# Second head pair's two weight sums: an accumulating DMA into a second load of one operand in place of VectorE additions

## The chip, the cores and the metric

The kernel runs on one core of one Trainium2 chip. A core has a matrix engine (TensorE, PE in the profile), three engines for element-wise work (VectorE or DVE, ScalarE or ACT, GpSimd or POOL), an engine that only issues transfers (SyncE or SP), and 16 DMA engines that move data between device memory and the core's on-chip memory. The metric is device time in microseconds (us) of one execution. It was measured in three runs of the kernel before: 846.02 us in the middle, 844.99 at the lowest, 846.65 at the highest.

## The reference

Two encoder layers over 512 tokens of 1024 channels, in float32. Both are: RMS norm, one wide input projection, an attention mixer, a gate, an output projection, and the residual added. Layer A, where the change stands, has dilated sliding-window attention with three dilation groups, merged by their softmax denominators:

```python
def mixer_a(hn, w_in, w_out, q_gain, k_gain, t5_bias):
    proj = hn @ w_in
    qkv = proj[..., :n_qkv].reshape(b, s, N_DIL_GROUPS, 3, N_HEADS, HEAD_DIM)
    gate = proj[..., n_qkv:]
    for g, (window, dilation) in enumerate(DILATED_PAIRS):
        q = rms_norm(qkv[:, :, g, 0], q_gain[g])
        k = rms_norm(qkv[:, :, g, 1], k_gain[g])
        v = qkv[:, :, g, 2]
        o, lse = dilated_group_attention(q, k, v, t5_bias[...], dilation, reach)
        ...
    alpha = jax.nn.softmax(jnp.stack(lses), axis=0)
    y = jnp.sum(alpha[..., None] * jnp.stack(outs), axis=0)
    y = y.reshape(b, s, BRANCH_WIDTH) * jax.nn.silu(gate)
    return y @ w_out
```

Inside `dilated_group_attention` the logits are `q k^T * scale + bias`, where the bias is a table over relative positions. Layer B does the same kind of work with a two-dimensional neighbourhood; it is not touched.

## The kernel before

**Weights.** The kernel's 16 heads are worked in eight pairs; `hc` counts them from 0. All projection weights lie in one packed array `in_w`. They come into on-chip tiles called `wraw`, 128 x 1024 float32 (512 KB), of which there are eight (`SLOTS`). Such a load is called a raw here. A raw is worked in two pieces of 512 columns, called jobs. For each job ACT casts the piece into a high part `wh`, then DVE or POOL subtracts it from the raw and makes the low part `wl`, and PE multiplies in three passes (`wh` by the high part of the activations, `wl` by the high part, `wh` by the low part). That is `splits()`, which runs a few jobs ahead of PE.

**The sums.** For the pairs 1 to 7 a part of the projection is done with products of sums, so that seven block products do the work of eight. Four weight blocks `b11`, `b21`, `b12`, `b22`, each of two raws (index 0 and 1), enter as they are and in these sums: `b11 += b12`, then `t2 = b11 + b22` (with `b11` already holding its sum), then `b12 += b22` and at last `t2 += b21`. The activations have sums of their own, `mixed`, with a high and a low part `mix_h` and `mix_l`. A sum with `+=` is a DMA that POOL issues with `accum_op=ALU.add` (`Plan.add`): it reads the operand from `in_w` and adds it into the `wraw` tile. The sum `t2 = b11 + b22` is a DVE addition of two tiles into a third (`Plan.sum`), 128 x 1024.

**The plan.** `Plan.mixed(hc)` writes down, for one pair, which raws are used at which job and at which job each sum is to be issued. `Plan.loads` then gives every raw that has an offset in `in_w` a job at which SP loads it: `lead` (12 jobs here) ahead of its first use, or later, when all eight slots are taken, at the job behind the last use of the raw whose slot comes free. Where a tile is to be written again, the loading DMA waits until the last reader of the slot has ended. The pair `hc == 1` is called `late` and has an order of its own (`b11`, gate, `b21`, `b11` again, `t2`, `b22`, `b12`, v, `t2` again).

**What sets the order.** PE's instructions stand in the order in which the program is written. The other engines are ordered by a scheduler at build time, except where the program holds an order. Each engine then works its list strictly from front to back: an instruction that waits holds up all behind it, and so does a DMA on the engine that issues it. SP issues the loads (`load`) and also the loads of the attention bias:

```python
def bias_a(hc):
    e0 = wk.tile([P, 2, 256], F32, tag="e0", name="e0", bufs=1)
    e12 = wk.tile([P, 4, 224], F32, tag="e12", name="e12", bufs=1)
    for hd in range(2):
        h = 2 * hc + hd
        syn.dma_start(e0[:, hd, :], ...)
        for g in range(2):
            syn.dma_start(e12[:, 2 * hd + g, :], ...)
```

These six transfers per pair (`e` in the profile, read from `l_d` in device memory) are stated in the order head 0, head 1. For the pair 0 they are needed when the attention's logits (`log`) are there: DVE adds the bias to the logits and keeps their extremes in `minima`, tile by tile, first for head 0 and then for head 1. After that come exponentials on ACT, transposes, and the values `vt`, which PE transposes (`tp`). All of pair 0's attention runs beside the projection of pair 1, whose weight sums are the ones that the change touches.

Two further small loads matter: `oh`, a one-hot table, with which PE makes the bias table (`pl`), and the stores `l_d` of that table, both on SP.

Of the kernel before, what the change touches and what calls it, by code (L numbers as in the profile page):

```python
# [46 lines left out]
def tile_hybrid_encoder(  # L47
# [49 lines left out]
    vec, act, pol, syn = (Ordered(e) for e in (nc.vector, nc.scalar, nc.gpsimd, nc.sync))  # L97
# [82 lines left out]
    class Plan:  # L180
# [28 lines left out]
        def add(self, at, dst, off):  # L209

            dst.used(at)
            src = lambda: w[:, off : off + dst.cols]
            self.sums.setdefault(at, []).append(
                lambda: pol.dma_start(dst.tile, src(), accum_op=ALU.add)
            )

        def mixed(self, hc):
            b, j = hc * A_HC, len(self.jobs)
            b11, b21, b12, b22 = ([self.raw(b + 2048 * n + 1024 * i) for i in range(2)] for n in range(4))
            gate = self.raw(b - A_HC + 1152 * KT)  # L220
            v = self.raw(b - A_HC + 1024 * KT)
            t2 = [self.raw(None) for _ in range(2)]
            late = hc == 1
            order = (b11, gate, b21, b11, t2, b22, b12, v, t2) if late else (b11, gate, b21, v, b11, t2, b22, b12, t2)
            for part in order:
                for raw in part if isinstance(part, list) else [part]:
                    self.use(raw, 128 if raw in (gate, v) else 512)
            for i in range(2):
                self.add(j + 3 + 2 * i, b11[i], b12[i].off)
                self.sum(j + (9 if late else 11) + 2 * i, t2[i], b11[i], b22[i], vec)  # L230
                self.add(j + 15 + 2 * i, b12[i], b22[i].off)
                self.add(j + (17 if late else 19) + 2 * i, t2[i], b21[i].off)

# [58 lines left out]
    def splits():  # L292
        casts, queue, due = [], [], plan.loads(lead)
        for at, (raw, c, step, n) in enumerate(plan.jobs):
            first = at - start_jobs
            pool[0] = [0, 1] if first < 16 else [1, 2] if at < mixed_jobs else [2, 5]
            for r in due.get(at, ()):
                load(r)
            for add in plan.sums.get(at, ()):
                add()  # L300
            casts.append((cast(raw.tile[:, c : c + step], step), n))
            if len(casts) > 1:
                done, m = casts.pop(0)
                queue.append((*rest(*done), m))
            if len(queue) > 4:
                yield queue.pop(0)
        done, m = casts.pop(0)
        queue.append((*rest(*done), m))
        yield from queue
# [94 lines left out]
    def squares(v, ss, i, ns, on_act=True):  # L404
        sq = wk.tile([P, 512], F32, tag="sq", name="sq")[:, : ns * 64]
        if on_act:
            act.activation(sq, v, AF.Square)
        else:
            pol.tensor_mul(sq, v, v)

        def add():
            vec.tensor_reduce(
                ss[:, i * ns : (i + 1) * ns], sq.rearrange("p (a b) -> p a b", b=64), axis=AX.X, op=ALU.add
            )

        later_on(800, add) if held[0] else add()
# [270 lines left out]
    def main_a(hc):  # L687
# [50 lines left out]
        for n, acc, first, put in ((0, c, True, put_v), (1, b, True, put_u), (3, c, False, put12), (2, b, False, put22)):  # L738
            yield "mix", n
            yield from product(acc, mixed(n), first, put, ("q", hc - 1) if n == 0 else None)  # L740
# [794 lines left out]
```

## Time and profile before

| what | value |
|---|---|
| median of the runs (lowest to highest) | 846.02 us (844.99 to 846.65) |
| the profiled execution's own time | 846.23 us |
| its span in the trace | 844.3 us |
| PE busy | 827.9 us, 98% |
| DVE, ACT, POOL busy | 632.8, 507.7, 292.0 us |
| granted TensorE clock | 1.00 |
| loads and other transfers on SP's queue (q1) | 108.39 MB, 41.8% of 16 engines' span |
| accumulating DMAs on POOL's queue (q0) | 42 of 512 KB, 22.02 MB, 15.2% |

Times in the rows are microseconds from the start of the span. A row of a timeline has start, duration, engine, line, operation, output and inputs with their shape and, in square brackets, how long the engine was idle before and on what it waited. Nearly every row has line 85, because a helper records each call there; the names of the tiles tell them apart, and numbers of buffers are left out. "SPq" and "POOLq" are the queues' issuing work, not the transfer itself. A row of windows gives a stretch, then its length, then busy time of PE, PEld (weight load), DVE, ACT and POOL, the clock, the share of the DMA engines and GB/s. A row of the DMA view has 40 equal slices with the busy share of the 16 engines in tenths, and under it the GB/s. A line of a queue has packets, MB and the share of 16 engines' time.

### The profile page before, as it was taken

What the parts mean: (1) busy time and instruction counts of PE and PEld (TensorE: products, weight loads), DVE (VectorE), ACT (ScalarE), POOL (GpSimd) and SP (SyncE); (2) the same over time, 40 slices, a digit from 0 to 9 for tenths busy, and PEclk for the clock granted to TensorE, in tenths of its full rate; (3) what the DMA queues carried; (4) which work ended last, traced back from release to release, by engine and by line L of the source; (5) the groups of instructions that cost most, each with busy time, mean ns of one, the idle gap of its engine ahead of it and who ended that gap; (6) DMA issues with size and microseconds to landing.
All of it is one profiled execution on the core that took longest, in us unless ns stands there. A gap on an engine that the chain in (4) does not pass through costs nothing.

```text
span 844.3 us, 18126 instructions
## 1 busy us (share of the span) xinstructions
PE 827.9 (98%) x6611; PEld 684.9 (81%) x6611; DVE 632.8 (75%) x1653; ACT 507.7 (60%) x1066; POOL 292.0 (35%) x259
## 2 busy tenths in 40 slices
PE   8999999999999999999999999999999999999998
PEld 6877878878877878878888887789998898889786
DVE  7899997897996886896796876466668767776742
ACT  7657766846846846747747738454546664666440
POOL 5042343543533533533533524213123222322201
PEclk9999999999999999999999999999999999999999
DMA  9426765676687776785676554473265456634212
GB/s 339 144 57 165 194 154 150 141 168 197 133 181 211 159 174 173 164 210 134 157 180 176 105 183 144 152 235 114 91 191 164 130 145 180 179 129 114 85 51 101
DMA packets 56169, 131.97 MB, mean 156 GB/s; under 512 B 7184, under 2 KB 24528, under 8 KB 55952
## 3 DMA queue, kind: packets, MB, share of 16 engines
q1 hardware_dynamic: 49456, 108.39, 41.8%
q0 software_dynamic: 6048, 22.02, 15.2%
q8 instruction: 52, 0.85, 0.4%
q10 hardware_dynamic: 576, 0.41, 0.2%
q14 instruction: 37, 0.30, 0.1%
HBM read 111.73 MB, written 11.72 MB: 146 GB/s over the span
## 4 chain that ended last, share of the span: by engine, by line
PE 76%; ACT 9%; DVE 8%; issue 3%; DMA 3%; POOL 1%; SPq 0%; DVEq 0%; ACTq 0%; POOLq 0%
PE acc L324 63%; PE log L324 5%; PE o L324 4%; ACT p L85 4%; PE tp L328 3%; DVE wl L85 2%; ACT wh L85 1%; DVE na L85 1%; DMA wraw<-in_w 1%; DVE rawq L85 1%; DMA yr<-y_d 1%; ACT rawk L85 1%; DVE gt L85 1%; DVE p L85 1%; DMA pt<-in_xt 1%
## 5 line engine op out<-in xcount | busy, mean ns | idle before, releaser
L85 POOL TENSOR_TENSOR wl<-wraw,wh 128x512 fp32r<-128x512 f32 (+1 forms) x153 | 198.2, 1296 | 434.5 <-PE acc L324 223.2
L85 ACT CAST wh<-wraw 128x512 fp32r<-128x512 f32 (+1 forms) x360 | 209.3, 593 | 194.1 <-PE acc L324 154.9
L85 DVE TENSOR_TENSOR wl<-wraw,wh 128x512 fp32r<-128x512 f32 (+1 forms) x207 | 158.3, 768 | 44.5 <-PE acc L324 33.4
L324 PE MATMUL acc<-wh,hn_h 128*128 128x384 f32 (+1 forms) x488 | 185.5, 380 | 2.9 <-DVE gt L85 1.7
L324 PE MATMUL acc<-wl,hn_h 128*128 128x384 f32 (+1 forms) x488 | 177.2, 363 | 3.1 <-DVE wl L85 3.1
L324 PE MATMUL acc<-wh,hn_l 128*128 128x384 f32 (+1 forms) x488 | 176.9, 362 | 0.0
L85 ACT ACTIVATE p<-p,mn 128x256 f32<-128x256 f32 (+2 forms) x248 | 137.6, 584 | 32.3 <-DVE mn L85 32.3
L324 PEld LDWEIGHTS acc<-wh,hn_h 128*128 128x128 f32 x488 | 91.7, 188 | 21.4 <-issue 7.0
L324 PEld LDWEIGHTS acc<-wl,hn_h 128*128 128x128 f32 x488 | 91.9, 188 | 12.1 <-DVE wl L85 4.9
L324 PEld LDWEIGHTS acc<-wh,hn_l 128*128 128x128 f32 x488 | 91.6, 188 | 9.5
L324 PE MATMUL acc<-wh,mix_h 128*128 128x512 f32 x224 | 89.2, 398 | 0.0
L324 PE MATMUL acc<-wl,mix_h 128*128 128x512 f32 x224 | 87.6, 391 | 0.0
L324 PE MATMUL acc<-wh,mix_l 128*128 128x512 f32 x224 | 87.4, 390 | 0.0
L324 PE MATMUL acc<-hn_h,wh 128*128 128x512 f32 x192 | 79.0, 412 | 0.3 <-ACT rawb L85 0.2
L324 PE MATMUL acc<-hn_h,wl 128*128 128x512 f32 x192 | 75.1, 391 | 0.0
L324 PE MATMUL acc<-hn_l,wh 128*128 128x512 f32 x192 | 75.0, 391 | 0.0
L85 DVE STREAM_TRANSPOSE pt<-p 128x512 f32<-128x512 f32 (+1 forms) x60 | 40.6, 687 | 23.7 <-ACT p L85 23.6
L85 DVE TENSOR_REDUCE ss<-sq 128x4 f32<-128x256 f32 (+1 forms) x96 | 46.1, 501 | 11.0 <-POOL sq L85 5.9
L324 PE MATMUL acc<-y_h,wh 128*128 128x512 f32 x128 | 51.9, 406 | 0.5 <-ACT gt L85 0.5
L324 PEld LDWEIGHTS acc<-wh,mix_h 128*128 128x128 f32 x224 | 42.1, 188 | 10.0 <-issue 1.6
L324 PE MATMUL acc<-y_h,wl 128*128 128x512 f32 x128 | 50.0, 391 | 0.0
L324 PE MATMUL acc<-y_l,wh 128*128 128x512 f32 x128 | 49.9, 390 | 0.0
(148 smaller groups left out, 1361.5 us busy)
## 6 DMA issues: line engine op xcount, KB each, us to landing
wraw<-in_w SPq DMA_DIRECT2D x95, 512.0 KB
wraw<-in_w POOLq DMA_DIRECT2D x42, 512.0 KB, 7.0
wraw<-in_w SPq DMA_DIRECT2D x38, 384.0 KB
pt<-pt SPq DMA_DIRECT2D x106, 64.0 KB
td<-tr SPq DMA_DIRECT2D x24, 224.0 KB
pt<-td SPq DMA_DIRECT2D x24, 224.0 KB
e<-l_d SPq DMA_DIRECT2D x32, 112.0 KB
e<-l_d SPq DMA_DIRECT2D x16, 128.0 KB
```

Of the source, the lines that this page charges most:

```text
L85: m = f(*args, **kw)
L324: nc.tensor.matmul(o, l, r, **kw)
L328: nc.tensor.transpose(o, i, ident)
```

## The change

For the pair 1 alone, `t2` is no longer an empty tile into which DVE writes the sum. It is given the offset of `b22`, so SP loads `b22` a second time, straight into `t2`'s tile. Then an accumulating DMA on POOL's queue adds `b11` (which holds `b11 + b12`) to it. The source of that DMA is a tile in on-chip memory, not `in_w`: `add` takes a raw instead of an offset for that. The other six pairs keep the DVE sum.

```diff
         def add(self, at, dst, off):
 
             dst.used(at)
-            src = lambda: w[:, off : off + dst.cols]
+            if isinstance(off, Raw):
+                off.used(at)
+                src = lambda: off.tile
+            else:
+                src = lambda: w[:, off : off + dst.cols]
             self.sums.setdefault(at, []).append(
                 lambda: pol.dma_start(dst.tile, src(), accum_op=ALU.add)
             )
...
-            t2 = [self.raw(None) for _ in range(2)]
             late = hc == 1
+            t2 = [self.raw(b22[i].off if late else None) for i in range(2)]
...
             for i in range(2):
                 self.add(j + 3 + 2 * i, b11[i], b12[i].off)
-                self.sum(j + (9 if late else 11) + 2 * i, t2[i], b11[i], b22[i], vec)
+                if late:
+                    self.add(j + 9 + 2 * i, t2[i], b11[i])
+                else:
+                    self.sum(j + 11 + 2 * i, t2[i], b11[i], b22[i], vec)
                 self.add(j + 15 + 2 * i, b12[i], b22[i].off)
                 self.add(j + (17 if late else 19) + 2 * i, t2[i], b21[i].off)
```

Since `b22` is no longer an operand of the sum at job `j + 9`, its first use is at its own jobs, from `j + 18`. The plan's loads shift with that. With `j = 16`, counted in jobs: before, `b22[0]` and `b22[1]` are loaded at 13 and 17, `b12[0]` and `b12[1]` at 25 and 27. After, `t2[0]` and `t2[1]` are loaded at 13 and 15, `b12[0]` and `b12[1]` at 19 and 23, and `b22[0]` and `b22[1]` at 25 and 27, of which the last takes the slot that `b21[1]` leaves after job 25.

On SP, in the stretch from the loads ahead of `oh` to the bias of pair 0 (`e`) and the loads behind it, the program before has:

```order
L85 DMA wraw<-in_w 128x1024 x5
L85 DMA oh<-in_onehot 32x896
L85 DMA wraw<-in_w 128x1024
L85 DMA l_d<-mk 16x384 x4
L85 DMA l_d<-mk 16x512
L85 DMA wraw<-in_w 128x1024 x2
L85 DMA e_730<-l_d 128x1x256
L85 DMA e_731<-l_d 128x1x224 x2
```

And the changed program, in the same stretch:

```order
L85 DMA wraw<-in_w 128x1024 x6
L85 DMA oh<-in_onehot 32x896
L85 DMA wraw<-in_w 128x1024
L85 DMA l_d<-mk 16x384 x4
L85 DMA l_d<-mk 16x512
L85 DMA wraw<-in_w 128x1024 x3
L85 DMA e_732<-l_d 128x1x256
L85 DMA e_733<-l_d 128x1x224 x2
```

One weight load more stands ahead of `oh`, and one more ahead of the six loads of `e`: behind `l_d` there are now `b12[1]`, `b22[0]` and `b22[1]`, where `b12[0]` and `b12[1]` were.

On POOL, around the issue of the accumulating DMAs of pair 1, the difference of the two programs is:

```order
 L85 TENSOR_TENSOR mix_l<-mixed,mix_h 128x1024
 L85 TENSOR_TENSOR hn_l<-pt,hn_h 128x512
-L85 DMA wraw<-in_w 128x1024 x2
+L85 DMA wraw<-in_w 128x1024
+L85 DMA wraw<-wraw 128x1024 x2
+L85 DMA wraw<-in_w 128x1024
 L85 TENSOR_TENSOR wl<-wraw,wh 128x512
 L85 DMA wraw<-in_w 128x1024 x2
```

The two new DMAs (`wraw<-wraw`) stand between `b11[1] += b12[1]` and `b12[0] += b22[0]`, which followed each other before; the three accumulations of `t2 += b21` and `b12[1] += b22[1]` still come behind the next `wl`.

On DVE, in the stretch of pair 1's `wl` pieces, two rows go, the two sums; around the first of them the difference is:

```order
 L85 SCALAR_TENSOR_TENSOR rs<-na,rs 128x16
 L85 TENSOR_TENSOR rawk<-rawk,rs 128x256
-L85 TENSOR_TENSOR wraw<-wraw 128x1024
 L85 TENSOR_TENSOR wl<-wraw,wh 128x512
 L85 TENSOR_TENSOR mixed<-mixed,pt 128x1024
```

The `wl` now follows directly on the key rows' scaling (`rawk`). The rest of DVE's list keeps its order, and so do the lists of ACT and PE.

## The prediction

> **What bounds the kernel now.** I read the page's busy table first, then TensorE's (PE's) waits around the change.
>
> ```profile
> PE 827.9 (98%) x6611; PEld 684.9 (81%) x6611; DVE 632.8 (75%) x1653; ACT 507.7 (60%) x1066; POOL 292.0 (35%) x259
> ...
> PE acc L324 <- DVE wl L85: 1.3, 1, 1.3
> PE tp L328 <- ACT vt L85: 0.7, 1, 0.7
> ```
>
> PE is busy for 827.9 of 844.3 us, so the time is PE's work plus its few waits. The last two rows are all its waits between 30 and 160 us, where the two sums stand: 1.3 us for a `wl` (the low part of a weight piece, made by VectorE, DVE), then 0.7 us at 112 us. The timelines of PE, DVE and ACT show the first:
>
> ```profile
> 73.59 0.50 PE L324 MATMUL acc<-wl,hn_h 128*128 128x512 f32 x1 [1.31 <-DVE wl L85]
> ...
> 67.64 1.22 DVE L85 TENSOR_TENSOR wraw<-wraw 128x1024 f32<-128x1024 f32 x1
> 68.77 0.69 DVE L85 TENSOR_TENSOR wl<-wraw,wh 128x512 fp32r<-128x512 f32 x1
> 69.37 1.22 DVE L85 TENSOR_TENSOR mixed<-mixed,pt 128x1024 f32<-128x1024 f32 x1
> 70.51 0.76 DVE L85 TENSOR_TENSOR rawk<-rawk,rs 128x256 f32<-128x256 f32 x2
> 71.71 1.23 DVE L85 TENSOR_TENSOR mix_l<-mixed,mix_h 128x1024 fp32r<-128x1024 f32 x1 [0.45 <-ACT mix_h L85]
> 72.85 0.68 DVE L85 TENSOR_TENSOR wl<-wraw,wh 128x512 fp32r<-128x512 f32 x1
> 73.79 1.22 DVE L85 TENSOR_TENSOR wraw<-wraw 128x1024 f32<-128x1024 f32 x1
> 84.81 0.69 DVE L85 TENSOR_TENSOR rawq<-acc,rawk 128x512 f32<-128x512 f32 x1 [1.44 <-PE acc L324]
> ...
> 70.63 1.05 ACT L85 CAST mix_h<-mixed 128x1024 fp32r<-128x1024 f32 x1 [5.15 <-DVE mixed L85]
> ```
>
> DVE works without a gap from the first sum (67.64) to the `wl` of 72.85 that PE waits for; the 0.45 us for `mix_h` hangs on DVE's own `mixed` (69.37), so it moves with the rest. The second sum (73.79) stands behind that `wl`, and DVE waits for PE at 84.81.
>
> **The change, part by part.**
>
> *The two DVE sums go.* The first pushes the `wl` of 72.85 by 68.77 − 67.64 = 1.13 us. Without it PE waits 1.31 − 1.13 = 0.18 us: a gain of 1.13 us, 1.31 at most. The second frees DVE in a stretch that ends in a wait for PE, so I cost it at nothing.
>
> *Two accumulating DMAs come* (`t2 += b11`), on POOL's queue.
>
> ```profile
> 62.62 1.78 POOL L85 DMA_DIRECT2D wraw<-in_w  x2
> 78.91 2.18 POOL L85 TENSOR_TENSOR wl<-wraw,wh 128x512 fp32r<-128x512 f32 x1 [14.52 <-ACT wh L85]
> 81.39 1.76 POOL L85 DMA_DIRECT2D wraw<-in_w  x2 [0.30 <-POOL wl L85]
> 84.75 0.87 POOL L85 DMA_DIRECT2D wraw<-in_w  x1 [0.30 <-POOL wl L85]
> ...
> 79.49 0.65 ACT L85 CAST wh<-wraw 128x512 fp32r<-128x512 f32 x1
> ...
> DMA to landing us min/median/max: 5.7/7.7/9.0
> ...
> q1 hardware_dynamic: 49456, 108.39, 41.8%
> q0 software_dynamic: 6048, 22.02, 15.2%
> ...
> wraw<-in_w POOLq DMA_DIRECT2D x42, 512.0 KB, 7.0
> ```
>
> The row of landing times is that of POOL's DMAs between 55 and 95 us. The new ones go between the two issues of 62.62. Issuing costs POOL 0.9 us each; the second must also wait for the sum in `b11[1]` to land, 62.62 + 5.7 to 7.7 = 68.3 to 70.3, and `b12[0] += b22[0]` is queued behind it. POOL then has nothing until 78.91 (14.52 us idle), which hides both. ACT's cast of the second `t2` is that of 79.49, 78.4 with the gain; issued at 69 to 70 and 7.7 to 9.0 us under way, the sum lands at 77 to 79, which is about in time.
>
> On the 16 DMA engines an accumulation costs 15.2% × 844.3 / 42 = 3.06 us. Its source is now SBUF instead of HBM, which no row shows: as low as a plain load, 41.8% × 844.3 us × 0.524 / 108.39 MB = 1.7 us, or as high as twice the row, 6.1 us. I take 3.06: the destination and the adding there are those of the row, only the source is another.
>
> *The second load of `b22` moves other loads.* `t2` now loads early, where `b22` did, and `b22` itself is first used at its own jobs, nine jobs later, so its loads go down SP's order.
>
> ```profile
> 29.79 0.42 SPq L85 DMA_DIRECT2D oh<-in_onehot  x1
> 38.49 0.33 SPq L85 DMA_DIRECT2D wraw<-in_w  x1
> 65.69 8.08 SPq L85 DMA_DIRECT2D e<-l_d  x6
> ...
> L85 SPq DMA_DIRECT2D wraw<-in_w x5: 328/328/351, 65.1 to 91.6; - x5
> ...
> 46.03 1.68 PE L324 MATMUL pl<-oh,t 32*16 32x384 f32 x6
> ```
>
> `oh` comes behind the load that waited until 38.49: issued at 38.8, it has 7.2 us until PE reads it at 46.03. That is hidden (plain data of 1.7 us). What is not clearly hidden is the bias: the six `e` loads followed the weight load of 65.1 directly. Now they stand behind one more weight load, `b22[1]`, and its slot is the one that `b21[1]` leaves, that is, after the `wl` of 72.85, then at about 72.4. SP holds the `e` loads for that: 7 us later at issue.
>
> **What the seven microseconds meet.** The DMA view from 60 to 80 us, in slices of 0.5 us, and DVE's first readers of `e`:
>
> ```profile
> DMA  0000000093699999899999942222222222289973
> GB/s 0 0 0 0 0 0 0 0 74 41 106 213 188 213 188 188 197 262 246 270 295 279 301 170 98 92 98 82 86 95 92 94 94 95 96 210 324 351 215 100
> ...
> e<-l_d SPq DMA_DIRECT2D x4, 112.0 KB
> e<-l_d SPq DMA_DIRECT2D x2, 128.0 KB
> ...
> 86.63 0.29 DVE L85 CUSTOM_DVE_ANT_0 p<-log,e 128x192 f32<-128x192 f32 x1
> 88.34 0.29 DVE L85 CUSTOM_DVE_ANT_0 p<-log,e 128x192 f32<-128x192 f32 x1
> 112.27 0.66 PE L328 MATMUL tp<-ident,vt 128*128 128x128 f32 x4 [0.73 <-ACT vt L85]
> ```
>
> From 64.0 to 72.0 the engines are full with two accumulations and two loads; by the prices above that is 9.5 us of work, done in 8.0, a factor of 0.84. Then follow eleven slices at two tenths and 93 GB/s: the `e` loads keep only part of the engines busy, and 704 KB (0.72 MB) at 93 GB/s take 7.7 us. Today they are through soon after 80, and nobody waits.
>
> After the change four accumulations and three loads stand there: 12.2 + 5.1 = 17.3 us, times 0.84 to 1, so the queues run dry at 78.6 to 81.3; I take 79.5. From 81.39 POOL issues the next three accumulations, whose packets begin 1.4 us after issue (62.62 to 64.0), at 82.8. That leaves 3.3 of the 7.7 us: 2.6 of the six `e` loads. The rest meet three accumulations of 3.06 us, to about 92. What such a meeting does is shown at the next pair (115 to 140 us, slices of 0.625 us; SP and POOL rows):
>
> ```profile
> DMA  5744456498999999996312327978899953222000
> ...
> 117.30 0.88 POOL L85 DMA_DIRECT2D wraw<-in_w  x1 [3.19 <-PE acc L324]
> 118.15 10.44 SPq L85 DMA_DIRECT2D e<-l_d  x6
> 120.60 0.88 POOL L85 DMA_DIRECT2D wraw<-in_w  x1 [1.11 <-DVE wl L85]
> ...
> L85 SPq DMA_DIRECT2D e<-l_d x6: 579/1016/5072, 118.2 to 126.7; - x6
> ```
>
> The engines are full from 120.0 to 126.3, one issue is held for 5.07 us, and the low stretches that mark `e` alone come at 126.9 to 130 and again from 136: issued at 118.15, these loads move mostly after the accumulations. I therefore let the remaining 3.4 `e` loads run mainly after 92: less about one that slips between, 2.4 × 1.28 = 3.1 us, last data at 95.1. A lone accumulation lands 5.7 us after issue, of which 1.4 + 3.06 are start and data, so completion adds 1.2; for `e` I count nothing, since less than a slice is at stake against the 3 us of spread above.
>
> DVE needs the last three `e` at 88.34. It gets them at about 95.1: 6.8 us later than before, the gain of 1.13 already used up in waiting. From there softmax work on DVE and ACT leads to `vt`, for which PE waits at 112.27 already today. How much could DVE make up?
>
> ```profile
> 95.00:112.00 17.00, 16.54 (x110) 13.24 (x99) 15.52 (x45) 14.92 (x30) 6.68 (x5) 1.00 0.45 134
> ```
>
> It is the third figure of busy time: 15.52 of 17.00, so at most 1.5 us. Taking the delay whole: 846.23 + 6.8 = 853.0 for the profiled execution (span 844.3 and 1.9 around it); it stands 0.2 above the median of the runs, 846.02, so against that 852.8.
>
> The Trainium skill ("DMA: Bandwidth & Descriptors", Queues, rings and completion order) says that each DMA engine takes turns between queues packet by packet. The rows above agree: an accumulation's packets have 22.02 MB / 6048 = 3.6 KB, a row of `e` 0.9 to 1.0 KB (224 or 256 numbers), so in equal turns `e` gets a fifth, and the sum stays near 852.8.
>
> Were the engines shared by time instead, `e` would run at half speed, 3.3 us alone and 8.8 us shared, to 91.6, and the sum would be 846.02 + 3.3 = 849.3.
>
> **The rivals.**
>
> *The bias comes in time (not slower).* The place is DVE's row at 88.34, the price of the `e` delay then zero, and 846.02 − 1.13 = 844.9 remains. It decides if the `e` data start by 79.5: 7.7 us before 87.2, with the later accumulations not stopping them. For it: three quarters of the engines are idle while `e` runs; an SBUF source at 1.7 us would end the four accumulations and loads at 64.0 + 14.6 × 0.84 = 76.3. Against it: from 82.8 the next accumulations run either way, so `e` would have to begin by 82.8 − 7.7 = 75.1, and `b22[1]`, ahead of it in the same queue, is issued only at 72.4 and shares each turn.
> The same page of the Trainium skill (Anatomy of one DMA) fits 2.0 us plus bytes over 436 GB/s to such a DMA, an estimate of 3.2 us from issue to landing. The row has 5.7 at least, so the measurement decides; by the page's figure this rival would hold.
>
> *Only the tail is caught.* If one or two `e` loads are left at 82.8, they finish inside or just behind the accumulations, at 90 to 92: 846.02 + 1.7 to 3.7, about 848.7.
>
> *SBUF to SBUF is slow.* At 6.1 us each the two sums end about 6 us later, at 85; the cast of the second `t2` waits (its `wl` feeds PE), all six `e` loads meet the next accumulations and the last ends at about 92 + 6 + 2: 846.02 + 11.7, about 857.7.
>
> *The gain is larger.* The whole 1.31 us and the 0.73 us at 112.27, by a DVE that runs earlier throughout: 844.0, faster.
>
> **How the numbers follow.** A difference of 0.2% (1.7 us) is about what a measurement of this kernel can tell from none. Forecast 0.55; only the tail 0.11; SBUF slow 0.12; in time 0.16; larger gain 0.06. Of the tail case, which begins at 847.7, I give 0.02 to no change, so faster is 0.06, same 0.18, slower 0.76. The forecast's own range goes from 849.3 (sharing by time) to 855 (queues dry only at 81.3, which leaves 1.8 us more of `e` behind 92). Both signs matter, so the full range goes from 844.7 to 856.5 and leaves out most of the larger gain and the worse half of the slow case.
>
> **What would show it.** In the changed kernel's trace: PE's wait near 73 falls below 0.3 us (right), or stays (another input of that `wl` was late). SP issues `e` from about 72 to 73; earlier means my slot is wrong. The DMA view stays at nine tenths until 78 to 81, with the two-tenths stretch short and broken. DVE shows a wait for DMA ahead of the readers of `e` at 85 to 87 and above all at the second tile, 5 us or more, and PE a new wait by 112 of nearly that size. If DVE has no wait there, the forecast is wrong and the time is near 844.9; if ACT waits for DMA at a `wh` cast near 79, SBUF accumulation is the slow part.

## The result, and the profile after

The changed kernel takes 856.71 us (median of four runs, 855.97 to 858.84); the kernel before, with one run more beside it, 845.64 us. The ratio is 1.0127 (95% interval 1.0112 to 1.0142): slower by 1.3%, some 10.7 us. The forecast was 852.8 us, slower by 0.8%; the measured time lies 0.2 us above the upper end of the range. The profiled execution took 856.29 us with a span of 854.5, so 10.2 us of span are to be explained.

Where PE waits between 30 and 160 us, and the rows of PE's timeline:

```profile
PE acc L331 <- DVE wl L85: 9.6, 2, 9.4
PE tp L335 <- ACT vt L85: 0.4, 1, 0.4
...
72.14 0.49 PE L331 MATMUL acc<-wl,hn_h 128*128 128x512 f32 x1 [0.16 <-DVE wl L85]
101.11 0.80 PE L331 MATMUL acc<-wl,mix_h 128*128 128x512 f32 x1 [9.42 <-DVE wl L85]
122.95 0.66 PE L335 MATMUL tp<-ident,vt 128*128 128x128 f32 x4 [0.40 <-ACT vt L85]
```

The wait near 73 us is nearly gone, 0.16 us instead of 1.31. In its place PE waits 9.42 us at 101.11 for another `wl`, and the row for `vt` comes at 122.95 where it came at 112.27. DVE's timeline tells why that `wl` is late:

```profile
84.92 0.29 DVE L85 CUSTOM_DVE_ANT_0 p<-log,e 128x192 f32<-128x192 f32 x1
87.48 0.48 DVE L85 CUSTOM_DVE_ANT_1 p<-log,e,mn 128x256 f32<-128x256 f32 x1 [2.26 <-DMA e<-l_d]
93.99 0.36 DVE L85 CUSTOM_DVE_ANT_0 p<-log,e 128x192 f32<-128x192 f32 x1 [5.34 <-DMA e<-l_d]
98.21 0.48 DVE L85 CUSTOM_DVE_ANT_1 p<-log,e,mn 128x256 f32<-128x256 f32 x1 [3.86 <-DMA e<-l_d]
100.37 0.69 DVE L85 TENSOR_TENSOR wl<-wraw,wh 128x512 fp32r<-128x512 f32 x1
```

Three readers of the bias wait for its loads, 11.5 us together, and the `wl` that PE needs (100.37) stands behind them in DVE's list. Where the loads were, by SP's and POOL's timelines and the DMA view from 60 to 80 us (slices of 0.5 us):

```profile
38.56 0.42 SPq L85 DMA_DIRECT2D oh<-in_onehot  x1
62.94 9.54 SPq L85 DMA_DIRECT2D wraw<-in_w  x3
72.65 8.68 SPq L85 DMA_DIRECT2D e<-l_d  x6
...
62.89 1.20 POOL L85 DMA_DIRECT2D wraw<-wraw  x1
70.03 0.85 POOL L85 DMA_DIRECT2D wraw<-wraw  x1 [5.94 <-DMA wraw<-in_w]
70.57 1.21 POOL L85 DMA_DIRECT2D wraw<-in_w  x1
77.46 1.29 POOL L85 TENSOR_TENSOR wl<-wraw,wh 128x512 fp32r<-128x512 f32 x1 [5.69 <-PE acc L331]
79.06 1.77 POOL L85 DMA_DIRECT2D wraw<-in_w  x2 [0.30 <-POOL wl L85]
...
DMA  0000000397959999999999999999999999999954
q0 software_dynamic: 576, 2.10, 56.5%
```

SP issues `e` from 72.65, not 65.69. The DMA engines are full without a break from about 66 to 79.0. The next accumulations are issued at 79.06, and the same view from 80 to 100 us has no long stretch at two tenths before 97:

```profile
DMA  2587486999999999999952966999999964222222
```

Last, what the long wait does to PE, in windows (the clock is the figure behind the five busy times):

```profile
91.00:94.00 3.00, 0.69 (x3) 0.22 (x2) 0.01 (x1) 0.00 (x0) 0.00 (x0) 1.00 0.97 264
94.00:97.00 3.00, 0.00 (x0) 0.00 (x0) 0.36 (x2) 0.00 (x0) 0.00 (x0) 0.51 0.86 244
103.00:106.00 3.00, 3.00 (x75) 2.44 (x72) 2.23 (x6) 3.00 (x8) 0.48 (x1) 0.50 0.31 117
106.00:109.00 3.00, 3.00 (x10) 2.36 (x10) 2.84 (x8) 1.72 (x4) 2.17 (x2) 0.72 0.37 89
109.00:112.00 3.00, 3.00 (x15) 2.48 (x14) 2.96 (x6) 2.98 (x7) 1.30 (x1) 1.00 0.80 254
...
PE 830.6 (97%) x6611; PEld 686.8 (80%) x6611; DVE 630.7 (74%) x1651; ACT 508.1 (59%) x1066; POOL 292.9 (34%) x261
```

The granted clock halves during the wait and is back at 1.00 only by 109. PE's busy time grows from 827.9 to 830.6 us for the same 6611 matmuls. The account of the span: waits for `wl` −1.31 + 0.16 + 9.42 = +8.27, busy time +2.7, the wait for `vt` −0.33; together +10.6 of the measured +10.2, the rest being small waits elsewhere.

### The profile page after: what moved, and what is told of

It is laid out like the page before. It is cut to its first block, busy times and chain, and to the rows that moved or that the text cites. A ratio compares the mean times of both kernels' runs of the same rounds, so it can differ in the third digit from the quotient of the medians.

```text
span 854.5 us, 18137 instructions
## 1 busy us (share of the span) xinstructions
PE 830.6 (97%) x6611; PEld 686.8 (80%) x6611; DVE 630.7 (74%) x1651; ACT 508.1 (59%) x1066; POOL 292.9 (34%) x261
## 4 chain that ended last, share of the span: by engine, by line
PE 72%; ACT 8%; DVE 7%; DMA 5%; issue 3%; SPq 2%; POOL 1%; DVEq 0%; ACTq 0%
PE acc L331 60%; PE log L331 4%; PE o L331 4%; ACT p L85 4%; PE tp L335 3%; DMA wraw<-in_w 3%; SPq L85 2%; DMA e<-l_d 2%; DVE wl L85 2%; ACT wh L85 1%; DVE na L85 1%; ACT rawk L85 1%; DVE p L85 1%; DVE tr L85 1%; DMA pt<-in_xt 1%
## 5 line engine op out<-in xcount | busy, mean ns | idle before, releaser
L331 PEld LDWEIGHTS acc<-wh,hn_h 128*128 128x128 f32 x488 | 91.6, 188 | 21.4 <-issue 6.8
L331 PEld LDWEIGHTS acc<-wh,hn_l 128*128 128x128 f32 x488 | 91.6, 188 | 9.5
L331 PEld LDWEIGHTS acc<-wl,mix_h 128*128 128x128 f32 x224 | 42.5, 190 | 18.4 <-DVE wl L85 10.2
L331 PEld LDWEIGHTS acc<-wh,mix_h 128*128 128x128 f32 x224 | 42.3, 189 | 10.2 <-issue 1.8
```

What stands on the lines that cost most here:

```text
L331: nc.tensor.matmul(o, l, r, **kw)
```

## The experiments

The theory was the prediction's: the bias loads are late because they stand behind `b22[1]`'s load on SP, and then starve under accumulating DMAs. The rivals were that the added DMA work alone does it, that late issue alone does it, and that the accumulations before 80 us do it and not those behind. The first four kernels ran on one chip, where the kernel before had 846.40 us (25 runs, 843.71 to 847.91); the last four on one where it had 846.33 us (28 runs). Whole-run times on these chips vary by some 2 us either way, so effects near 1 us are read from the traces.

### Bias loads early, both accumulations kept

```diff
         yield from bias_lines()
+        st["e", 0] = bias_a(0)
         yield "wait", ("rawk", 0), 1000
...
         yield from mix()
-        st["e", 0] = bias_a(0)
```

> The changed kernel, with the six bias loads of pair 0 issued right behind the stores of the bias table (about 51 us) instead of behind the load of b22[1]; DVE, ACT, PE and POOL keep their order, the four accumulations stay. Theory (the bias loads are late because of their place on SP, and then starve under the accumulations): no wait of DVE for e, PE's wait near 72 us stays at 0.2 us and that near 91 us is gone, the time is 845.6 - 1.1 = 844.5 us (843.8 to 845.5). Rival (the two added accumulations are too much DMA work by themselves, so something else, a cast of t2 or a weight load, comes late): 848 us or more, with a wait for a DMA on ACT or DVE between 75 and 95 us.

Measured: 846.38 us, ratio 1.0003 (0.9987 to 1.0019). SP's timeline, PE's row near 72 us, and PE's waits from 30 to 160 us:

```profile
54.05 4.15 SPq L85 DMA_DIRECT2D e<-l_d  x6
62.86 42.77 SPq L85 DMA_DIRECT2D wraw<-in_w  x11
...
72.06 0.49 PE L331 MATMUL acc<-wl,hn_h 128*128 128x512 f32 x1 [0.16 <-DVE wl L85]
...
PE tp L335 <- ACT vt L85: 0.7, 1, 0.7
PE acc L331 <- DVE wl L85: 0.2, 1, 0.2
```

With `e` issued at 54.05, ahead of the long wait for a slot (the loads behind it begin at 62.86), all of the loss is gone, though the four accumulations still run. ACT and DVE wait for no DMA. That refutes the rival of added DMA work, and shows the gain at its place: 0.16 us of PE's wait. The whole-run median is 1.9 us above what I expected, and outside the range I gave. A second set of this kernel, in five rounds, settles what that is worth.

> The kernel with the early bias loads once more, in more rounds. Theory (both kernels' waits as its trace shows them: the span of 842.2 against 844.3 us, PE without the 1.3 us wait): 0.1 to 0.25% faster than before. Rival (something else in single executions gives it back): no difference.

Measured: 845.10 us, ratio 0.9994 (0.9981 to 1.0006). The gain of 1.1 us cannot be told from nothing in whole runs.

### The same loads, the sums by DVE

```diff
                 if late:
-                    self.add(j + 9 + 2 * i, t2[i], b11[i])
+                    self.sum(j + 9 + 2 * i, t2[i], b11[i], t2[i], vec)
```

> The changed kernel's loads (t2 loaded with b22, b22 loaded later, the bias loads behind it on SP), but the two sums by DVE again, so no accumulation is added. Theory (late issue and added accumulations are both needed): bias issued at about 74 us, its data from 75.5 us, 7.7 us long, nearly all of it ahead of the next accumulations (82.8 us); DVE waits for e under 2 us, PE's wait near 73 us is 1.3 us as before, the time is 845.6 us (844.8 to 847.5). Rival (the late issue alone is enough): DVE waits for e by 5 us or more, 851 to 856 us.

Measured: 851.94 us (845.85 to 854.14 in ten runs), ratio 1.0054 (1.0028 to 1.0080). My expectation missed. DVE's rows for the readers of `e`, the issues of `e` on SP, and POOL's row, of an execution of 854.13 us:

```profile
88.14 0.29 DVE L85 CUSTOM_DVE_ANT_0 p<-log,e 128x192 f32<-128x192 f32 x1
94.92 0.48 DVE L85 CUSTOM_DVE_ANT_1 p<-log,e,mn 128x256 f32<-128x256 f32 x1 [6.48 <-DMA e<-l_d]
...
L85 SPq DMA_DIRECT2D e<-l_d x6: 510/618/2977, 73.9 to 77.1; - x6
...
81.19 1.76 POOL L85 DMA_DIRECT2D wraw<-in_w  x2 [0.30 <-POOL wl L85]
```

Four of the bias loads are in time, and of the last two at least one is not: one that misses the gap costs the whole length of the accumulations behind it (issued from 81.19), 6.5 us. My sum had the last load through at 83.2, so nearly on the edge; the trace has one issue held for 2.98 us, to 80.1, which puts it over. What held it is open. Ten runs between 845.9 and 854.1 us fit a race that is sometimes won, but a trace of a fast one was not taken. So late issue alone is mostly enough for a loss, about half as large (ratio 1.0054 against 1.0127); the rest comes with the two added accumulations.

### Fewer accumulations behind

```diff
-                self.add(j + (17 if late else 19) + 2 * i, t2[i], b21[i].off)
+                self.add(j + (21 if late else 19) + 2 * i, t2[i], b21[i].off)
```

> The changed kernel, but the two accumulations t2 += b21 planned four jobs later, so that of the three that met the bias loads from 80 us on, one (b12[1] += b22[1]) is left. Theory (the bias is held by those three): the last reader of e waits until about 91 us instead of 98 us, DVE's waits for e go from 11.5 us to 3 to 5 us, the time is 848 to 850 us. Rival (the bias is held by the four accumulations before 80 us alone): no difference, 855 to 857 us.

Measured: 852.31 us, ratio 1.0076 (1.0057 to 1.0094). DVE's waits for `e`, and the row where PE waits for the `wl`:

```profile
DVE p L85 <- DMA e<-l_d: 5.3, 3, 2.9
...
95.29 0.79 PE L331 MATMUL acc<-wl,mix_h 128*128 128x512 f32 x1 [3.45 <-DVE wl L85]
```

DVE's wait halves and 4 us come back, with the four accumulations ahead of 80 us untouched. So a large part of the starving is done by those behind, as the theory has it. The last reader starts at 92.40 instead of 98.21. The time is 2.3 us above the upper end of my figure. The clock, which falls here too (last section), can account for about 1 us of that: the last reader is 3.7 us later than in the kernel before, PE's row for `vt` 4.7 (117.00). The rest is open.

### One sum by DMA, the other by DVE

```diff
-            t2 = [self.raw(b22[i].off if late else None) for i in range(2)]
+            t2 = [self.raw(b22[i].off if late and i == 0 else None) for i in range(2)]
...
-                if late:
+                if late and i == 0:
                     self.add(j + 9 + 2 * i, t2[i], b11[i])
                 else:
-                    self.sum(j + 11 + 2 * i, t2[i], b11[i], b22[i], vec)
+                    self.sum(j + (9 if late else 11) + 2 * i, t2[i], b11[i], b22[i], vec)
```

> The changed kernel with the first of the two sums by accumulating DMA, the second by DVE as before; the bias loads still stand behind three weight loads. Theory: one accumulation of 3 us less, so the queues run dry at about 76.5 us and some five of the six bias loads are through by 82.8 us; the last ends behind the accumulations at 91 to 93 us, DVE waits 3 to 5 us at one row, PE's wait near 73 us is 0.2 us; 848 to 850 us. Rival (either accumulation alone does not matter): 844.5 us.

Measured: 845.35 us, ratio 0.9994 (0.9981 to 1.0006). SP's rows:

```profile
51.48 14.07 SPq L85 DMA_DIRECT2D wraw<-in_w  x3
65.73 11.87 SPq L85 DMA_DIRECT2D e<-l_d  x6
```

My figure of 848 to 850 missed, and the trace shows why: I had counted three weight loads ahead of `e`, but not asked what the third waits for. With one sum on DVE `b22[1]` is still loaded early for it, the last of the three loads takes a slot that is free sooner, so `e` is issued at 65.73, as in the kernel before. PE's wait near 72 us is 0.2 us. It is the wait for the slot that matters, not the number of loads.

### PE kept busy during the wait

```diff
+AT, FILL = 109, 9
...
         matmul(o, lh, rh, start=first, stop=False, **kw)
+        nth[0] += 1
+        for _ in range(FILL if nth[0] == AT else 0):
+            nc.tensor.matmul(o[:1], zero, rh.bitcast(F32), start=False, stop=False, **kw)
         matmul(o, lh, rl, start=False, stop=False, **kw)
...
+    zero = warm
+    vec.memset(warm, 0.0)
```

> The changed kernel with nine matmuls more (a column of zeros against a weight piece, added into the running sum, so they change nothing) just ahead of the matmul that waited 9.42 us; they need nothing that is late and fill the larger part of that wait. Theory (part of the loss is the granted clock, which was 0.5 to 0.7 from 94 to 109 us and made PE's work 2.7 us longer, 830.6 against 827.9 us): the clock stays at 1.00 and the time is 856.7 - 2.7 = 854.0 us (853 to 855). Rival (PE's slower matmuls lie beside DVE's and ACT's chain and cost nothing): 856 to 857.5 us.

Measured: 854.64 us, ratio 1.0097 (1.0083 to 1.0110) against 1.0127 (1.0112 to 1.0142) of the changed kernel, which was measured in another set of runs: 2.5 us less by the ratios, though the two intervals nearly touch. PE's rows (a filling matmul shows as two records), DVE's last reader of `e`, a window and the busy line:

```profile
91.78 7.88 PE L342 MATMUL acc<-wh,warm 128*1 128x512 f32 x18
100.91 0.50 PE L332 MATMUL acc<-wl,mix_h 128*128 128x512 f32 x1 [1.24 <-DVE wl L86]
121.63 0.65 PE L336 MATMUL tp<-ident,vt 128*128 128x128 f32 x4 [1.48 <-ACT vt L86]
...
98.01 0.48 DVE L86 CUSTOM_DVE_ANT_1 p<-log,e,mn 128x256 f32<-128x256 f32 x1 [3.64 <-DMA e<-l_d]
...
100.00:105.00 5.00, 4.09 (x84) 3.20 (x85) 4.36 (x13) 4.04 (x9) 0.00 (x0) 1.00 0.36 118
...
PE 836.2 (98%) x6629; PEld 686.3 (80%) x6629; DVE 628.9 (74%) x1652; ACT 507.5 (59%) x1066; POOL 292.8 (34%) x261
```

And the last reader in the kernel before:

```profile
88.67 0.48 DVE L85 CUSTOM_DVE_ANT_1 p<-log,e,mn 128x256 f32<-128x256 f32 x1
```

The late `wl` still lets PE go on only at 100.91, but now at full clock; without the filling, busy time is 836.2 − 7.9 = 828.3 us, 2.3 us less than in the changed kernel. Not all of that reaches the end. In the changed kernel the last reader of `e` is 9.5 us later than in the kernel before, and PE's row for `vt` 10.7, so 1.1 us are added between the two. With the filling both are 9.3 to 9.4 us later (98.01 and 121.63) and nothing is added, but PE, now faster, waits 1.48 us for `vt` instead of 0.40. The two spans differ by 1.3 us (853.2 against 854.5). So in the traces the low clock costs 1.1 to 1.3 us on top of the wait, and 2.5 by the ratios of whole runs. The rest of PE's slower work lies beside DVE's and ACT's chain, as the rival has it.

### Other ways to the gain

With one sum by DMA and the bias early (both edits above together):

> One accumulating DMA for the first sum, the second sum on DVE, and the six bias loads right behind the stores of the bias table. Theory: PE's wait near 73 us falls to 0.2 us and no wait for e is possible, since e lands before 63 us: 0.13 to 0.25% faster than before (844 to 845 us where before has 846). Rival: no difference.

Measured: 845.20 us, ratio 0.9987 (0.9971 to 1.0003). PE's wait near 72 us is 0.2 us, nothing waits for `e`; the interval just reaches no change, so a version that beats the kernel before is not shown.

With the first sum made by POOL, in the kernel before:

```diff
-                self.sum(j + (9 if late else 11) + 2 * i, t2[i], b11[i], b22[i], vec)
+                self.sum(j + (9 if late else 11) + 2 * i, t2[i], b11[i], b22[i], pol if late and i == 0 else vec)
```

> The kernel before with the first of the two sums made by POOL (a tensor addition of 128 x 1024) instead of DVE; no load and no DMA moves. POOL had nothing to do from 64.4 to 78.9 us. Theory (the gain of the change is DVE's 1.13 us ahead of the wl that PE waits for, and any engine that is free gives it): PE's wait near 73 us falls from 1.3 to 0.2 us, 0.13% faster, 844.9 us where before has 846.0. Rival (an addition on POOL slows DVE's instructions beside it): DVE's rows between 64 and 68 us are longer and the wait stays above 0.6 us; no difference.

Measured: 848.17 us, ratio 1.0020 (1.0008 to 1.0032). POOL's sum, DVE's two `wl` beside it, PE's row behind its wait for a `wl`, a window and the busy line; and then the same two `wl` in the kernel before:

```profile
63.51 2.62 POOL L85 TENSOR_TENSOR wraw<-wraw 128x1024 f32<-128x1024 f32 x1
63.99 3.29 DVE L85 TENSOR_TENSOR wl<-wraw,wh 128x512 fp32r<-128x512 f32 x2
74.65 0.50 PE L324 MATMUL acc<-wl,hn_h 128*128 128x512 f32 x1 [2.16 <-DVE wl L85]
...
76.00:79.00 3.00, 3.00 (x11) 2.31 (x10) 3.00 (x7) 3.00 (x8) 0.00 (x0) 0.51 0.41 114
...
PE 830.9 (98%) x6611; PEld 687.7 (81%) x6611; DVE 633.5 (75%) x1652; ACT 508.5 (60%) x1066; POOL 293.4 (35%) x260
```

```profile
63.80 1.28 DVE L85 TENSOR_TENSOR wl<-wraw,wh 128x512 fp32r<-128x512 f32 x2
```

The rival holds: beside POOL's addition two of DVE's subtractions take 3.29 us instead of 1.28, more than the 1.13 us that DVE is spared, and PE's wait grows from 1.3 to 2.2 us. Behind that wait the clock falls as well, to 0.51 from 76 to 79 us, and PE's busy time is 830.9 instead of 827.9 us.

## Why the prediction was right or wrong

- **The gain.** The DVE sum gone, PE's wait should fall to 0.18 us; it is 0.16. The second sum brought nothing, as said. Right.
- **The new accumulations on POOL.** The second was to wait for a landing at 68.3 to 70.3; issued at 70.03. POOL's idle time hid it, and ACT did not wait at the cast of `t2`. By the share of q0 from 60 to 80 us, four accumulations took 56.5% × 20 / 4 = 2.8 us each; two of them read on-chip memory. I had taken 3.06 for the unknown price, with 6.1 as the upper bound. Right, so the case of a slow source is out.
- **`oh` later.** Issued at 38.56; PE did not wait for it. Right.
- **The bias loads later.** Forecast from about 72 to 73, measured 72.65. Right, and the early bias shows that it is the cause.
- **The queues run dry at 79.5.** Measured about 79.0. Right.
- **The next accumulations at 81.39.** Wrong, and the first step that failed. I moved DVE's readers by the gain, but left POOL's issue where it was. In the trace POOL's `wl` ahead of it starts 1.45 us earlier (77.46 against 78.91) and takes 1.29 instead of 2.18 us, so the accumulations are issued at 79.06, 2.3 us earlier. The gap of 3.3 us in which I let 2.6 of the six loads through shrank to about 1.5 us (79.0 to 80.5, with the 1.4 us from issue to packets). Why POOL's `wl` was shorter is open.
- **The last bias data at 95.1.** Measured 98.21, 3.1 us later. The mechanism was right, the term was mis-sized; the smaller gap, 1.8 us less, is the nearest explanation, and no run isolates it or the rest.
- **The way to PE.** I led the delay through the softmax to `vt` at 112. It reached PE before that: a `wl` of the weights in work stands in DVE's list behind the readers of `e`, and PE stopped after 91.7 us. DVE's last reader is 98.21 − 88.67 (the kernel before, same row) = 9.5 us late, PE's row for `vt` 10.7. That the size of the forecast carried over to this other path is in part luck: the `wl` hangs on the same readers.
- **The clock.** Not in the sum at all. By the kept-busy experiment it costs 1.1 to 1.3 us in the traces, 2.5 by the whole runs.
- **The range.** It ended at 856.5, too low by 0.2. With both missing terms the sum is 6.8 + 3.1 + 1.1 = 11.0 us, against 10.7 measured in whole runs and 10.2 in the span of the trace.

Of the rivals, "the bias comes in time" describes the early-bias kernel, not this one; turns packet by packet fit the last reader at 98.21 better than shared time, by which `e` would have ended at 91.6, but no experiment separates the two.

## What to carry to other kernels

An added load can cost more by what it holds up than by its bytes: look at what stands behind it on the issuing engine, and what the load itself must wait for, here a buffer slot. Small transfers that need few DMA engines should be issued before heavy accumulating DMAs, since missing the gap can cost the length of the whole next batch, 6.5 us here. When a step is made earlier, move everything behind it in the forecast, also the work that competes with the late transfer.

## What the runs showed of the hardware that was not expected

A PE wait of a few microseconds also slows the matmuls behind it. With waits for a `wl` of 2.16, 3.45, 4.81 and 9.42 us (the sum on POOL, fewer accumulations behind, the sums by DVE, the changed kernel) the granted clock fell to about 0.50, and PE's busy time rose by 3.0, 3.1, 4.1 and 2.7 us over 827.9; in these four the rise does not grow with the wait. Some 1 us of it can be chance, since two executions of the kernel with the early bias, with no such wait, have 829.1 and 828.0 us. It is busy time, of which only a part reaches the end, as the kept-busy experiment shows. The first case stands above; a window and the busy line of the second:

```profile
97.00:100.00 3.00, 3.00 (x77) 2.44 (x73) 2.42 (x6) 3.00 (x7) 0.29 (x1) 0.50 0.61 199
...
PE 831.0 (98%) x6611; PEld 687.3 (81%) x6611; DVE 627.0 (74%) x1651; ACT 507.9 (60%) x1066; POOL 295.7 (35%) x261
```

And of the third:

```profile
97.00:100.00 3.00, 2.19 (x12) 1.54 (x14) 2.85 (x10) 2.14 (x5) 0.00 (x0) 0.50 0.36 108
...
PE 832.0 (98%) x6611; PEld 687.6 (81%) x6611; DVE 631.0 (74%) x1653; ACT 508.1 (60%) x1066; POOL 291.8 (34%) x259
```

After the 1.31 us wait of the kernel before the clock stayed at 1.00:

```profile
73.00:76.00 3.00, 2.41 (x12) 1.74 (x12) 3.00 (x6) 3.00 (x7) 0.00 (x0) 1.00 0.27 91
```

The Trainium skill ("TensorE: Matmul & The Clock Gate", Part 1) has half the clock after an idle window of about 3.4 us. The wait of 1.31 us and those from 3.45 us on agree with that, the 2.16 us do not: here a shorter wait was enough. In the changed kernel, too, the clock fell some 2.3 us after PE stopped (1.00 in the window up to 94, 0.51 from 94 to 97, PE idle from 91.7). Where between 1.31 and 2.16 us the border lies, and whether it is the same each time, no run shows.

An accumulating DMA between two on-chip tiles costs the DMA engines about the same as one from device memory. With two of each, q0's packets took 56.5% of 20 us, 11.3 us of all 16 engines; with the two from device memory alone (the kernel before, same stretch) 29.4%, 5.9 us. That is 2.9 us for one from device memory and (11.3 − 5.9) / 2 = 2.7 us for one between on-chip tiles.
